# Hybrid decoder trunk on one core: 16 of the 22 inner tiles of the FFN down projection by seven block products, with parts of the inner layer worked out in the up projection and kept in DRAM

## The chip, the core and the metric

The kernel runs on one core of a Trainium2 chip. The core has a matrix engine (TensorE, PE in the profile; its weight loads are listed apart as PEld), VectorE (DVE), ScalarE (ACT), GpSimd (POOL), and SyncE (SP), which here issues nearly all DMAs, in order, from one queue. Each engine takes its own instructions strictly in the order in which the built program has them, and waits on semaphores for others. The metric is the device time of one execution in microseconds (us).

## What is computed

One decoder layer on 1024 tokens of width 1024: three token mixers in parallel with a merge and an output projection, and then the sub-layer that the change touches, the gated MLP:

```python
h = rms_norm(x, pre_ffn_norm[l])
u = causal_dwconv(h @ ffn_w_up[l], ffn_conv_w[l], ffn_conv_b[l])
gate, val = jnp.split(u, 2, axis=-1)
f = (jax.nn.gelu(gate, approximate=True) * val) @ ffn_w_down[l]
x = x + rms_norm(f, post_ffn_norm[l])
```

The inner width is 11 x 1024 / 4 = 2816, that is 22 tiles of 128 channels. Everything is float32.

## The kernel before

Activations stand with channels on partitions and tokens along the free axis, in two halves of 512 tokens (h = 0, 1). A float32 product is made of three matmuls: each operand is split into a rounded high part and the rest (`hi`, `lo`), and hi x hi, hi x lo and lo x hi are summed in PSUM. A split of an activation is a copy on ACT (`hi`) and a subtraction on DVE (`lo`); a split of a weight has its subtraction on POOL.

**Up projection.** Each inner tile f needs a gate tile and a value tile. The first four tiles go by plain products (`up_half`). For the other 18, `up_pair` takes gate and value tile (two blocks of output channels) by two token halves and two halves of the contraction as a 2 x 2 block product, and makes it with seven block products for eight (Winograd's form of Strassen's scheme): `weights7` works out sums of weight blocks on POOL and splits them on ACT and POOL, `product` issues the 12 matmuls of one of the seven, `snap` copies an intermediate PSUM bank to SBUF on ACT. The sums of the input blocks were made once before (`combos`). One pair is 84 matmuls. Then `conv` (three taps, ACT and DVE), GELU on ACT, and `gated` (DVE) make one inner tile of 128 x 512 for each token half, which is stored to DRAM (`m_d`, line 1528).

**Down projection.** Inner tiles come back from DRAM in chunks of 4, 4, 4, 4, 2 and 4 (`DOWN`). `m_split` loads a tile into a staging buffer (lines 1589 and 1595) and splits it (1601, 1602); `down` makes, for each of the eight output tiles j and both token halves, the plain product over the chunk's tiles, with weights from `load_w` (270 to 273), and adds the PSUM bank to one of 16 sums in SBUF (`acc`, line 1617; the first chunk copies, 1615). The last chunk is done by token ranges, with the final norm and residual.

The first chunk's tiles are loaded inside the last pair. The recorded program is put into its final order by a scheduler that goes by modelled times: it interleaves products of neighbouring pairs and stages, and gives each engine its fixed order. A buffer of a pool is taken in the order in which the program asks for it, once its last reader has been placed. PSUM has six banks for these stages (`dense`).

Of the kernel before, what the change touches and what calls it, by code (L numbers as in the profile page):

```python
# [23 lines left out]
NFF = 22  # L24
# [68 lines left out]
def layout(a):  # L93
# [31 lines left out]
    for i, (c0, c1) in enumerate(TM_CHUNKS):  # L125
# [15 lines left out]
    dn = g["ffn_w_down"]  # L141

    dns = [units(dn[c * 128:(c + n) * 128], ar(DM)) for c, n in DOWN]
    out.update(
        xT=np.ascontiguousarray(x.T), wfm=wfm, pv=np.ascontiguousarray(pv),
# [7 lines left out]
        wb_nsa=units(g["w_br_nsa"], ar(DM)), wo=units(g["w_out"], ar(DM)),  # L153
        wup=units(up, fch), **{f"wdn{i}": d for i, d in enumerate(dns)})
# [29 lines left out]
W_BUFS = (3, 4, 4)  # L184
U_BUFS = 4
OSQ = 6

N_FIRST = 4
# [1168 lines left out]
def tail_stage(nc, tc, es, env):  # L1357
# [152 lines left out]
    def snap(ps):  # L1510
        s = up_.tile([128, 512], F32, name="snap", bufs=5)
        act(s, ps, AF.Copy)
        return s

    m_d = E.scratch("m_d", [NFF * 128, T])

    def conv(u, h, ps, st):
# [3 lines left out]
        st[s, h] = up_.tile([128, 512], F32, name=f"u{s}")  # L1521
        E.conv(st[s, h], h, ps, [pvc(PV_FW, 3 * u + 2 - d) for d in range(3)], pvc(PV_FB, u), st["halo", s])
        if s == 0:
            act(st[0, h], st[0, h], AF.Gelu_apprx_tanh)

    def gated(f, h, st):
        V.tensor_tensor(st[0, h], st[0, h], st[1, h], op=OP.mult)
        nc.sync.dma_start(m_d[f * 128:(f + 1) * 128, hs(h)], st[0, h])

# [7 lines left out]
    def up_pair(f, rhs, between=None):  # L1537
# [7 lines left out]
        V.tensor_tensor(y, y, s1, op=OP.add)  # L1545
        conv(2 * f, 0, y, st)
        E.product(x, w, rhs, 6, False)
        s2 = snap(x)
# [9 lines left out]
        conv(2 * f + 1, 0, z, st)  # L1558
        gated(f, 0, st)
        E.product(x, w, rhs, 3, False)  # L1560
        conv(2 * f + 1, 1, s7, st)
# [9 lines left out]
    rhs = {q: [None] * 4 for q in range(1, 8)}  # L1571
    later = []
    for k in range(4):
        quarters = [(1, h2[0, k]), (2, h2[0, k + 4]), (3, h2[1, k + 4])]
        lows = [rows[0][k], rows[1][k], rows[0][k + 4], rows[1][k + 4]]
        E.combos(*lows, V)
        for q, b in quarters:
            rhs[q][k] = b
        t2, t1, t4, t3 = lows
        for q, t in ((6, t2), (7, t3)):  # L1580
            rhs[q][k] = hi, lo = x_t(), x_t()
            act(hi, t, AF.Copy)
            V.tensor_tensor(lo, t, fl(hi), op=OP.subtract)
        later += [(5, k, t1, hi_t), (4, k, t4, lo_t)]

    for q, k, t, place in sorted(later, key=lambda x: (-x[0], x[1])):
        rhs[q][k] = hi, lo = place(), x_t()
# [4 lines left out]

    def m_tile(f, h, s):
        t = x_t(F32) if s is None else up_.tile([128, 512], F32, name=f"u{s}")
        nc.sync.dma_start(t, m_d[f * 128:(f + 1) * 128, hs(h)])
        return t

    def m_split(f, h):
        src = m_tile(f, h, None if f < DOWN[0][1] else f % 2)
        hi, lo = hi_t(), lo_t()  # L1600
        act(hi, src, AF.Copy)
        V.tensor_tensor(lo, src, fl(hi), op=OP.subtract)
        return hi, lo

# [3 lines left out]
    def down(ci, f0, nf, ms):  # L1608
        end = None
        for j in range(8):  # L1610
            pss = fm_unit(psd, load_w(A[f"wdn{ci}"][j], nf * 128), lambda k, h: ms[f0 + k, h], nf)
            for h, ps in enumerate(pss):
                a = acc[h][j]
                if ci == 0:
                    act(a, ps, AF.Copy)
                else:
                    end = V.tensor_tensor(a, a, ps, op=OP.add)
        return end


    ms0 = {}
    for f in range(N_FIRST, NFF):
        up_pair(f, rhs, (lambda: ms0.update(m_chunk(*DOWN[0]))) if f == NFF - 1 else None)

    last = len(DOWN) - 1
    tc.keep_in_program_order(nc.scalar.preload_act_table_set(E.TABLE))
    for ci, (f0, nf) in enumerate(DOWN[:last]):
        if ci == 0:
            acc = [[x_t(F32) for _ in range(8)] for _ in range(2)]
        i = down(ci, f0, nf, m_chunk(f0, nf) if ci else ms0)  # L1630
        if ci == last - 2:
            late = i

# [4 lines left out]
    def w_split(j, place):  # L1638
        ws.append(load_w(A[f"wdn{last}"][j], 512, place, up_.tile([128, 512], F32, name="snap", bufs=5)))

# [16 lines left out]
    def norm_rows(ss, W):  # L1657
# [6 lines left out]
        E.rsqrt_mean(rt[:, :n], v[:, :n], ps[:, :n], DM)  # L1664
        rb = up_.tile([128, 512], F32, name="u1")
        act(rb[:, :W].rearrange("p (n t) -> p n t", t=128), rt[:, :n, None].to_broadcast([128, n, 128]), AF.Copy)
# [14 lines left out]
    for s0, s1 in LAST:  # L1681
        h = s0 // 512
        s = slice(s0 - h * 512, s1 - h * 512)
        W = s1 - s0
        ss = up_.tile([128, 512], F32, name="u0")
        for j in range(8):
# [10 lines left out]
            else:  # L1697
                sq = up_.tile([128, 512], F32, name="snap", bufs=5)
                act(sq[:, :W], a, AF.Square)
# [23 lines left out]
```

## Time and profile before

| | us |
|---|---|
| time, median of 3 runs (2288.70 to 2292.17) | 2292.13 |
| the profiled execution | 2297.28 |
| its span, first to last instruction | 2295.5 |
| mean granted TensorE clock in it (share of full speed) | 0.985 |
| PE busy in the span | 2197.3 |
| DVE, ACT, POOL busy | 1346.2, 1164.9, 1184.5 |

The up projection's pairs run from about 1690 to 2040 us of the span, the down projection from about 2000 to the end; the two overlap in the last pair. A row of groups has the line, the engine, the operation, what it writes and reads by the program's names, the shapes and the count, then busy time in us, the mean duration of one in ns, and the idle time of the engine just before such instructions, with what ended it. A row of the timeline or of the chain of waits begins with the start and the duration in us. In rows of windows, each engine has its busy time and, in brackets, its instructions; then the granted clock, the busy share of the DMA engines and GB/s.

### The profile page before, as it was taken

What the parts mean: (1) busy time and instruction counts of PE and PEld (TensorE: products, weight loads), DVE (VectorE), ACT (ScalarE), POOL (GpSimd) and SP (SyncE); (2) the same over time, 40 slices, a digit from 0 to 9 for tenths busy, and PEclk for the clock granted to TensorE, in tenths of its full rate; (3) what the DMA queues carried; (4) which work ended last, traced back from release to release, by engine and by line L of the source; (5) the groups of instructions that cost most, each with busy time, mean ns of one, the idle gap of its engine ahead of it and who ended that gap; (6) DMA issues with size and microseconds to landing.
All of it is one profiled execution on the core that took longest, in us unless ns stands there. A gap on an engine that the chain in (4) does not pass through costs nothing.

```text
span 2295.5 us, 29758 instructions
## 1 busy us (share of the span) xinstructions
PE 2197.3 (96%) x10663; PEld 1755.3 (76%) x10663; DVE 1346.2 (59%) x2376; ACT 1164.9 (51%) x2185; POOL 1184.5 (52%) x853
## 2 busy tenths in 40 slices
PE   7999999998999999999999999999899999999997
PEld 7878889865665678878775678887678888878886
DVE  7765554268567526556536653359876777744346
ACT  6544443466756646667755421245545555553124
POOL 3676741246736733333347655446578888822213
PEclk9999999999999999999999999999999999999998
DMA  4233341320221011112253253334322222264212
GB/s 170 81 111 108 116 132 62 112 70 24 62 67 31 12 56 42 60 65 93 83 211 112 80 213 129 119 128 162 106 79 86 85 83 83 84 223 130 93 32 74
DMA packets 115349, 222.03 MB, mean 97 GB/s; under 512 B 28160, under 2 KB 42432, under 8 KB 115200
## 3 DMA queue, kind: packets, MB, share of 16 engines
q1 hardware_dynamic: 112608, 217.80, 28.0%
q10 hardware_dynamic: 2592, 2.32, 0.3%
q8 instruction: 84, 1.38, 0.2%
q14 instruction: 65, 0.53, 0.1%
HBM read 162.80 MB, written 57.28 MB: 96 GB/s over the span
## 4 chain that ended last, share of the span: by engine, by line
PE 77%; DVE 11%; ACT 5%; issue 3%; DMA 3%; POOL 2%; SPq 0%; DVEq 0%; ACTq 0%; POOLq 0%
PE dense L208 55%; PE ps_s L208 7%; PE ps_o L208 6%; PE ps_t L208 6%; PE ps_b L208 4%; POOL wlo L273 1%; DVE x L1484 1%; DVE mx L938 1%; DVE u L310 1%; DVE osq L1457 1%; DVE x L1589 1%; DMA wraw<-in_wdn 1%; DMA wraw<-in_wfm 0%; DVE x L1677 0%; DMA x<-in_xT 0%
## 5 line engine op out<-in xcount | busy, mean ns | idle before, releaser
L273 POOL TENSOR_TENSOR wlo<-wraw,whi 128x1024 fp32r<-128x1024 f32 (+2 forms) x134 | 266.5, 1989 | 444.1 <-ACT whi L272 435.4
L208 PE MATMUL dense<-hi,whi 128*128 128x512 f32 x816 | 308.2, 392 | 4.8 <-ACT whi L272 4.8
L208 PE MATMUL dense<-hi,wlo 128*128 128x512 f32 x752 | 289.3, 394 | 8.9 <-POOL wlo L273 7.9
L208 PE MATMUL dense<-lo,whi 128*128 128x512 f32 x688 | 269.3, 392 | 0.5 <-POOL lo L1497 0.5
L208 PE MATMUL dense<-h_hi,whi 128*128 128x512 f32 x656 | 263.8, 402 | 0.0
L208 PE MATMUL dense<-h_lo,whi 128*128 128x512 f32 x656 | 257.5, 393 | 0.0
L208 PE MATMUL dense<-h_hi,wlo 128*128 128x512 f32 x656 | 257.2, 392 | 0.0
L272 ACT ACTIVATE whi<-wraw 128x1024 fp32r<-128x1024 f32 (+2 forms) x134 | 116.1, 867 | 277.4 <-PE dense L208 228.8
L976 POOL TENSOR_TENSOR wT_lo<-wT,wT_hi 128x512 fp32r<-128x512 f32 x132 | 168.5, 1288 | 101.3 <-ACT wT_hi L975 93.2
L208 PEld LDWEIGHTS dense<-hi,whi 128*128 128x128 f32 x816 | 154.2, 189 | 39.5 <-ACT whi L272 6.9
L208 PE MATMUL dense<-x,uhi 128*128 128x512 f32 x552 | 177.3, 392 | 3.9 <-ACT x L584 2.4
L208 PEld LDWEIGHTS dense<-hi,wlo 128*128 128x128 f32 x752 | 142.1, 189 | 41.7 <-POOL wlo L273 10.4
L208 PEld LDWEIGHTS dense<-lo,whi 128*128 128x128 f32 x688 | 130.0, 189 | 28.6 <-POOL lo L1497 1.4
L208 PEld LDWEIGHTS dense<-h_hi,wlo 128*128 128x128 f32 x656 | 123.7, 189 | 26.7
L208 PEld LDWEIGHTS dense<-h_hi,whi 128*128 128x128 f32 x656 | 124.4, 190 | 23.8
L208 PEld LDWEIGHTS dense<-h_lo,whi 128*128 128x128 f32 x656 | 124.3, 189 | 22.5
L1180 POOL TENSOR_TENSOR s_lo<-sa,s_hi 128x512 fp32r<-128x512 f32 (+2 forms) x48 | 53.5, 1115 | 152.1 <-ACT s_hi L1179 152.1
L938 DVE TENSOR_REDUCE mx<-ps_t 128x1 f32<-128x384 f32 (+3 forms) x192 | 98.7, 520 | 47.7 <-PE ps_t L208 44.0
L208 PEld LDWEIGHTS dense<-x,uhi 128*128 128x128 f32 x552 | 103.7, 189 | 27.5 <-ACT x L584 3.6
L965 ACT ACTIVATE wT<-ps_s 128x512 f32<-128x512 f32 x132 | 78.4, 594 | 72.4 <-PE ps_s L208 67.1
L310 DVE SCALAR_TENSOR_TENSOR u<-dense,pv,u 128x510 f32<-128x510 f32 (+1 forms) x140 | 101.9, 737 | 7.8 <-ACT u L306 7.6
L521 POOL TENSOR_TENSOR ulo<-uf,uhi 128x1024 fp32r<-128x1024 f32 x30 | 72.5, 2418 | 63.4 <-ACT uhi L520 63.4
(514 smaller groups left out, 5690.9 us busy)
## 6 DMA issues: line engine op xcount, KB each, us to landing
wraw<-in_wfm SPq DMA_DIRECT2D x62, 512.0 KB, 3.7
wraw<-in_wup SPq DMA_DIRECT2D x52, 512.0 KB, 3.7
g_d<-gate_e SPq DMA_DIRECT2D x48, 256.0 KB, 2.1
s_d<-o SPq DMA_DIRECT2D x48, 256.0 KB, 2.0
ge<-g_d SPq DMA_DIRECT2D x24, 512.0 KB, 3.5
m_d<-u SPq DMA_DIRECT2D x44, 256.0 KB, 2.0
u<-m_d SPq DMA_DIRECT2D x36, 256.0 KB, 4.0
row<-s_d SPq DMA_DIRECT2D x16, 512.0 KB, 4.2
```

The costliest lines, as they stand in the source:

```text
L208: i = f(*a, **k)
L272: act(hi, raw, AF.Copy)
L273: (V if tiles else P).tensor_tensor(lo, raw, fl(hi), op=OP.subtract)
L310: V.scalar_tensor_tensor(o[:, d:], ps[:, :512 - d], taps[d], o[:, d:], op0=OP.mult, op1=OP.add)
L521: P.tensor_tensor(l24, f24, fl(h24), op=OP.subtract)
L938: V.tensor_reduce(mx[:, h, a, n:n + 1], pm[:, :w], axis=AX, op=OP.max)
L965: act(w.rearrange("p h q -> p (h q)"), pz, AF.Exp)
L976: P.tensor_tensor(lo, wf, fl(hi), op=OP.subtract)
L1180: (P if SB_SLO else V).tensor_tensor(s_lo[:, c0:], a[:, c0:], fl(s_hi[:, c0:]), op=OP.subtract)
L1457: eng.tensor_tensor(sums[0], sums[0], sq, op=OP.add)
L1484: e.tensor_tensor(o[j], o[j], x, op=OP.add)
L1589: V.tensor_tensor(lo, t, fl(hi), op=OP.subtract)
```

## The change

The inner tiles 4 to 19 are taken in four chunks of four tiles by seven block products each (`DOWN7`); the tiles 20, 21 and then 0 to 3 stay with plain products (`DOWN`). A chunk is worked in two halves of four output tiles (d = 0, 1). In a half, the 2 x 2 blocks are: two groups of output channels, two groups of contraction (even and odd inner tiles), and the two token halves. Weights are prepared by the same `weights7` as in the up projection, from a regrouped copy of the weight matrix, once per half.

The right-hand blocks of two neighbouring inner tiles (an even and an odd one, two token halves) have seven forms: three are tiles of the inner layer themselves, and four are differences and sums of them. `combine` works these four out on DVE in the up projection, after each odd tile, in two steps that are put off into the next pair, and stores them; the DRAM array `m7_d` holds seven blocks per two tiles for 16 tiles. `m_sets` loads and splits them in the order in which the products use them, straight into the buffer of the low part (`split_to`), without a staging buffer. Two sets of seven, one for each two tiles, make a chunk; of every third set, five of the seven blocks go to the pool `x`, which also holds the 16 sums.

`down7` issues, for each of the seven products and two output tiles, six matmuls, and adds the bank to one of the sums at once, one addition per product and bank; banks of three kinds (x, y, z; two each) keep running sums as in the scheme, so a bank is read by DVE and then written on. In the first chunk, the first write of each sum is a copy on ACT.

Counted in the built programs, PE has 96 matmuls fewer, DVE 104 instructions more, ACT 24, POOL 32 and the queue of SP 32 DMAs more. Buffers: `u0` 6 and `u1` 2 for 4 each, snapshots 6 for 5.

```diff
-DOWN = [(0, 4), (4, 4), (8, 4), (12, 4), (16, 2), (18, 4)]
+DOWN7 = [4, 8, 12, 16]
+DOWN = [(20, 2), (0, 4)]
...
+ORDER7 = (1, 2, 6, 7, 5, 4, 3)
...
     def gated(f, h, st):
-        V.tensor_tensor(st[0, h], st[0, h], st[1, h], op=OP.mult)
-        nc.sync.dma_start(m_d[f * 128:(f + 1) * 128, hs(h)], st[0, h])
+        m = st[0, h]
+        V.tensor_tensor(m, m, st[1, h], op=OP.mult)
+        if not in_pairs(f):
+            nc.sync.dma_start(m_d[f * 128:(f + 1) * 128, hs(h)], m)
+            return
+        if f % 2 == 0:
+            even[h] = m
+            q = {0: 1}.get(h)
+        else:
+            q = 2 + h
+        p = (f - DOWN7[0]) // 2
+        if q:
+            nc.sync.dma_start(m7_rows(p, q), m)
+        if f % 2 and h:
+            later.extend(combine(p, even[0], even[1], st[0, 0], m))
...
+    def combine(p, b11, b12, b21, b22):
+        t7, t6, t4 = [up_.tile([128, 512], F32, name="snap", bufs=SNAPS) for _ in range(3)]
+        def one():
+            V.tensor_tensor(t7, b12, b22, op=OP.subtract)
+            V.tensor_tensor(b12, b11, b12, op=OP.subtract)
+            for q, t in ((7, t7), (5, b12)):
+                nc.sync.dma_start(m7_rows(p, q), t)
+        def two():
+            V.tensor_tensor(t6, t7, b11, op=OP.subtract)
+            V.tensor_tensor(t4, t6, b21, op=OP.add)
+            for q, t in ((6, t6), (4, t4)):
+                nc.sync.dma_start(m7_rows(p, q), t)
...
+    def split_to(hi, lo, src):
+        nc.sync.dma_start(fl(lo), src)
+        act(hi, fl(lo), AF.Copy)
+        V.tensor_tensor(lo, fl(lo), fl(hi), op=OP.subtract)
+        return hi, lo
+    def m_sets(c):
+        sets = [{}, {}]
+        for n, q in enumerate(ORDER7):
+            for i, st in enumerate(sets):
+                if (2 * c + i) % 3 == 2 and n < 5:
+                    hi, lo = x_t(), x_t()
+                else:
+                    hi, lo = hi_t(), lo_t()
+                st[q] = split_to(hi, lo, m7_rows(2 * c + i, q))
+        return sets
+    def down7(c, sets):
...
+        for d in range(2):
+            w = E.weights7(wx, A[f"wds{c}"][d, 0], A[f"wds{c}"][d, 1], 512)
+            x, y, z = [[bank(), bank()] for _ in range(3)]
...
+            for q, ps, start, outs in ((1, x, True, ((0, 0, OP.add, True),)),
+                                       (2, y, True, ((0, 0, OP.add, False),)),
+                                       (6, x, False, ((0, 1, OP.subtract, True),)),
+                                       (7, z, True, ((1, 1, OP.add, True),)),
+                                       (5, x, False, ((1, 1, OP.subtract, False),)),
+                                       (4, z, False, ((0, 1, OP.add, False),)),
+                                       (3, x, False, ((1, 0, OP.add, True),))):
+                for n in range(2):
+                    product2(ps[n], q, n, start)
+                    for h, m, op, first in outs:
+                        end = add(h, 4 * d + 2 * n + m, ps[n], op, first)
```

More of the change, by code (lines that the diff above doesn't have):

```diff
@@ L1510, in snap @@
     def snap(ps):
-        s = up_.tile([128, 512], F32, name="snap", bufs=5)
+        s = up_.tile([128, 512], F32, name="snap", bufs=SNAPS)
         act(s, ps, AF.Copy)
@@ L1571, in tail_stage @@
     rhs = {q: [None] * 4 for q in range(1, 8)}
-    later = []
+    parts = []
     for k in range(4):
@@ L1591, in tail_stage, with split_in @@
     acc = []
[L1593 to L1596, printed above, removed]
-    def m_split(f, h):
[L1599 to L1603, printed above, removed]
+    def split_in(src):
+        hi, lo = hi_t(), lo_t()
+        return split_to(hi, lo, src)
@@ L1613, in down @@
                 a = acc[h][j]
[L1614 to L1621, printed above, removed]
-    for f in range(N_FIRST, NFF):
-        up_pair(f, rhs, (lambda: ms0.update(m_chunk(*DOWN[0]))) if f == NFF - 1 else None)
+                V.tensor_tensor(a, a, ps, op=OP.add)
+    acc = [[], []]
+    sets = []
+    for f in range(N_FIRST, NFF):
+        up_pair(f, rhs, (lambda: sets.extend(m_sets(0))) if f == NFF - 1 else None)
+    tc.keep_in_program_order(nc.scalar.preload_act_table_set(E.TABLE))
+    for c in range(len(DOWN7)):
+        if c:
+            sets = m_sets(c)
+        late = down7(c, sets)
     last = len(DOWN) - 1
-    tc.keep_in_program_order(nc.scalar.preload_act_table_set(E.TABLE))
     for ci, (f0, nf) in enumerate(DOWN[:last]):
[L1628 to L1632, printed above, removed]
+        down(ci, f0, nf, m_chunk(f0, nf))
     f0, nf = DOWN[last]
@@ L1638, in w_split @@
     def w_split(j, place):
-        ws.append(load_w(A[f"wdn{last}"][j], 512, place, up_.tile([128, 512], F32, name="snap", bufs=5)))
+        ws.append(load_w(A[f"wdn{last}"][j], 512, place, up_.tile([128, 512], F32, name="snap", bufs=SNAPS)))
     for k in range(nf):
```

57 lines of the change are left out of this document (49 added, 8 removed).

## The prediction

> **What bounds the kernel now.** I read first the page, then the windows over the feed-forward part, then the chain of waits in order of time, then who TensorE (PE) waits for.
>
> ```profile
> span 2295.5 us, 29758 instructions
> ```
> ```profile
> core 0: us, PE busy (x) PEld busy (x) DVE busy (x) ACT busy (x) POOL busy (x), PEclk, DMA share, GB/s
> 1950.00:2000.00 50.00, 50.00 (x222) 41.42 (x221) 33.90 (x45) 28.09 (x41) 40.86 (x24) 1.00 0.25 85
> 2000.00:2020.00 20.00, 16.96 (x68) 13.50 (x67) 14.44 (x21) 9.44 (x17) 12.86 (x9) 0.91 0.40 136
> 2050.00:2100.00 50.00, 47.56 (x209) 38.75 (x208) 18.21 (x27) 21.71 (x39) 11.64 (x9) 1.00 0.67 231
> ```
> ```profile
> 1699.38 293.12 PE dense L208 x1284
> ...
> 2007.08 3.52 DMA x<-m_d
> 2010.75 0.46 issue
> 2011.21 0.59 ACT snap L1512
> 2011.85 36.36 PE dense L208 x153
> ...
> 2049.62 11.88 DMA wraw<-in_wdn
> ```
> ```profile
> PE dense L208 <- ACT snap L1512: 5.1, 2, 3.0
> PE dense L208 <- ACT whi L272: 2.3, 1, 2.3
> ```
>
> In the up projection (1699 to 2012) and the down projection (to 2264) PE has no idle time in most windows. Only two stops show from 2000 on. At 2008.8 PE waits 3.0 us: a load of an inner tile is late, ScalarE (ACT), in order, takes the snapshot behind that tile's split. That window's granted clock is 0.91, so 0.09 x 20 = 1.8 us more are lost. In the window from 2050, after 36 inner-tile loads at once, a weight load takes 11.88 us and 13 of 222 matmuls are missing: 2.9 us. So fewer matmuls is the right thing to buy, if nothing else becomes late.
>
> **The price of a matmul.** One pair of the up projection is 84 matmuls and strictly periodic:
>
> ```profile
> 1897.12 0.39 PE L208 MATMUL dense<-hi,uhi 128*128 128x512 f32 x1
> 1916.16 0.39 PE L208 MATMUL dense<-hi,uhi 128*128 128x512 f32 x1
> 1918.88 0.61 PE L208 MATMUL dense<-x,uhi 128*128 128x512 f32 x2
> ```
> 19.04 us / 84 = 0.2267 us each (the 0.39 of a row overlaps its neighbours).
>
> **The change part by part.**
>
> *Removed:* 16 inner tiles cost 16 x 8 x 2 x 3 = 768 matmuls; seven products cost 4 chunks x 2 halves x 84 = 672. 96 x 0.2267 = **-21.8 us**, all on PE's path.
>
> *The weight-load stop after 2049* came from 36 loads in a burst; now the second half's weights load during the last pair and seven loads are spread over each half of 19 us, so I let it go: **-2.9** (bounds -2.9, and 0 if a burst comes back).
>
> *Weights.* 32 preparations of 128x512 become eight of the up projection's kind. VectorE (DVE) and GpSimd (POOL) rows of the up projection and the down projection:
>
> ```profile
> L310 DVE SCALAR_TENSOR_TENSOR u<-snap,pv,u 128x510 f32<-128x510 f32 x16 | 44.8, 2797 | 0.0
> L524 POOL TENSOR_TENSOR ulo<-uf,uhi 128x1024 fp32r<-128x1024 f32 x16 | 38.9, 2434 | 17.2 <-ACT uhi L523 17.2
> L521 POOL TENSOR_TENSOR ulo<-uf,uhi 128x1024 fp32r<-128x1024 f32 x16 | 38.4, 2400 | 27.7 <-ACT uhi L520 27.7
> L512 POOL TENSOR_TENSOR wlo<-wraw,whi 128x1024 fp32r<-128x1024 f32 x15 | 36.1, 2404 | 0.0
> L312 DVE SCALAR_TENSOR_TENSOR u<-halo,pv,u 128x2 f32<-128x2 f32 x31 | 35.8, 1156 | 0.0
> L310 DVE SCALAR_TENSOR_TENSOR u<-dense,pv,u 128x510 f32<-128x510 f32 x46 | 33.8, 735 | 0.0
> L522 POOL TENSOR_TENSOR uf<-wraw 128x512 f32<-128x512 f32 x16 | 28.0, 1748 | 0.0
> L517 POOL TENSOR_TENSOR uf<-wraw 128x512 f32<-128x512 f32 x16 | 25.6, 1601 | 1.2
> L519 POOL TENSOR_TENSOR uf<-uf,wraw 128x512 f32<-128x512 f32 x16 | 25.6, 1598 | 1.3
> L1527 DVE TENSOR_TENSOR u<-u,u 128x512 f32<-128x512 f32 x30 | 25.3, 843 | 1.8 <-ACT u L1524 0.4
> L526 POOL TENSOR_TENSOR alo<-wraw,ahi 128x512 fp32r<-128x512 f32 x16 | 20.8, 1302 | 0.0
> ```
> ```profile
> L1617 DVE TENSOR_TENSOR x<-x,dense 128x512 f32<-128x512 f32 x44 | 30.2, 687 | 71.8 <-PE dense L208 71.7
> L1602 DVE TENSOR_TENSOR lo<-u,hi 128x512 fp32r<-128x512 f32 x24 | 17.0, 748 | 11.3 <-ACT hi L1601 11.3
> ```
> POOL per half: 2.43 + 2.40 + 2.40 + 1.75 + 1.60 + 1.60 + 1.30 (L526) and once more for the sum of the same size (L518) = 14.8 us of 19.04. The up projection carries these and one more subtraction in the same time and PE is never short of weights there, so: 0. The cover is PE's own work on the half before; POOL has 4.2 us to spare, and what it took beyond that PE would pay in full, in each of eight halves.
>
> *DVE in the down projection.* A half has 14 adds from PSUM (a chunk of four tiles, twice a half's time and more, had 16; in the first chunk ACT makes 8 of 14 as copies) and about 7 splits: 14 x 0.69 + 7 x 0.69 = 14.5 us of 19.04, before waits. The waits are the question. The row L310 u<-snap takes 2.80 us where the same work from PSUM takes 0.74, and the timeline shows why:
>
> ```profile
> 1900.96 2.40 POOL L524 TENSOR_TENSOR ulo<-uf,uhi 128x1024 fp32r<-128x1024 f32 x1 [1.16 <-ACT uhi L523]
> ```
> ```profile
> 1900.27 0.21 DVE L312 SCALAR_TENSOR_TENSOR u<-halo,pv,u 128x1 f32<-128x1 f32 x1
> ...
> 1901.06 2.84 DVE L310 SCALAR_TENSOR_TENSOR u<-snap,pv,u 128x510 f32<-128x510 f32 x1
> ...
> 1909.97 1.02 DVE L1527 TENSOR_TENSOR u<-u,u 128x512 f32<-128x512 f32 x1
> 1914.86 0.70 DVE L1545 TENSOR_TENSOR dense<-dense,snap 128x512 f32<-128x512 f32 x1 [3.88 <-ACT snap L1512]
> ```
> The DVE operation with both inputs in SBUF ended half a microsecond after POOL's. Per pair such operations lose 2.06 (L310) + 2 x 0.95 (L312, 1.16 against 0.21) + 2 x 0.15 (L1527, 0.84 against 0.69) = 4.3 us. A split has both inputs in SBUF too; an add from PSUM has not. With the same 4.3 us, a half costs DVE 18.8 of 19.04 us: 99%. The order of instructions leaves 19 to 24 matmuls (4.3 to 5.4 us) between a bank's last matmul and its next, which absorbs most; I take 0.7 us per half over the six halves after the first chunk: **+4** (bounds: 0, as in the up projection, and, if each of seven splits waited 2.06, 9.8 x 6 = 59).
>
> The Trainium skill ("SBUF — State Buffer", section "Who interferes with whom") says that a VectorE instruction with two SBUF inputs and a GpSimd instruction that reads SBUF exclude each other, the later one blocked until the first ends. By that rule, these rows agreeing, it speaks against this change, and it is the second rival below.
>
> *Parts of the inner layer, in the up projection.* Per two pairs: four DVE operations (two SBUF inputs, 4 x 0.69 = 2.8 us) and three more stores. They stand right after the odd pair's second L1527, where DVE idles 3.88 us. What they make late: a snapshot buffer is now held until the store of the first part has landed, and the next pair's first snapshot waits for it on ACT, with the rest of ACT's work behind it. From 1910.99: wait for POOL 1.2, operation 0.6, issue 0.4, landing 2.0 to 4.0 (rows below), snapshot 0.6: 1915.8 to 1917.8; PE needs it at 1918.88. So 0 (bounds 0 and 8 x 1 us).
>
> ```profile
> m_d<-u SPq DMA_DIRECT2D x44, 256.0 KB, 2.0
> u<-m_d SPq DMA_DIRECT2D x36, 256.0 KB, 4.0
> ```
> Stores 44 to 68, loads of inner tiles 44 to 68, weights the same bytes in 16 loads: 7 x 256 KB + 2 x 512 KB per half is 2.8 MB in 19 us, 150 GB/s, where the windows show 231 served. The store of the parts goes ahead of a weight load on the DMA queue of SyncE (SP), 1.5 us at most; that load has more than 4 us of lead. ACT gets 24 instructions more, and is at 28 of 50 us: 0, as long as no load holds it up in order.
>
> *The stop at 2008.8 remains.* The first sets are loaded straight into freed tiles, no longer through two spare ones, but the last of these eight loads stands on SP's queue behind two stores of parts. From the end of L1527 (1910.99 in the cycle): two splits and two parts, 2.8; store and load issue 0.7; landing 2.6 to 4; split, weights and snapshot on ACT 0.63 + 1.06 + 0.58. That is 9.4, and PE wants the snapshot 5.2 us after (1916.16): about 4.0 idle for 3.0, with the clock loss as before: **+1.0** (bounds -4.8, it vanishes, and +4).
>
> *A new stop after the first chunk.* The third set keeps five of seven products' inputs in the tiles that also hold the 16 sums, and in the order of instructions their loads come after all sums are first written; on SP they are queued behind a load that waits for the first chunk's last but one matmul, and the next chunk's first matmul needs them. The path is that of 2007.08 to 2011.85, 4.8 us, and two issues (0.7) and DVE's split with the two ahead of it (1.5 to 2): **7.0 idle, 1.8 of clock: +8.8** (bounds 4.8, that path bare, and 13.2, the 11.88 us load and a split).
>
> The Trainium skill ("TensorE: Matmul & The Clock Gate", section "HAM oscillation — how this bites in real kernels") puts the halved clock behind idle stretches of more than about 3.4 us. The row above shows 0.91 after 3.0 us, so I charge it to both stops; by the page's bound the stop of before would have lost none, and the first of these two terms would be 2.8 for 1.0.
>
> **Sum:** -21.8 - 2.9 + 4 + 1.0 + 8.8 = -10.9. The profiled execution is 2297.28 us (span 2295.5 and 1.8 around it), 5.15 above the median 2292.13. 2297.3 - 10.9 = 2286.4; against the median, 2281.
>
> **Rivals.**
> 1. Most stops hide: the third set's loads land fast (4.8 + 1.8) and DVE keeps up (0): -21.8 - 2.9 + 1.0 + 6.6 = -17.1, 2275; with the 2008.8 stop gone too, 2269. For it: PE stayed busy in the up projection with POOL's load as high. Against: DVE was 68% busy there (33.90 of 50).
> 2. Slower: DVE becomes the bound in the down projection, because its splits and POOL's weights block each other. If a split waits 1.2 us on average instead of 0.6, a half takes 9.7 + 7 x 1.9 = 22.9 us, 3.9 over PE's: six halves 23 instead of 4, so -10.9 + 19 = +8: 2300. It decides from 1.0 us per split. For it: 2.80 us rows. Against: L1602 in the down projection now takes 0.75 (POOL only 23% busy there).
> 3. Snapshots in the up projection wait for stores, 1 to 2 us in each of eight: 2289 to 2297. Against: 1 to 3 us of room, above.
>
> **How the numbers follow.** Forecast (2274 to 2288) 0.5; rival 1, 0.2; rival 2 in full 0.12, and half of it (2288 to 2297) 0.1; rival 3, 0.08. A measurement tells about 0.2%, 4.6 us, from no change. Faster by more: 0.5 + 0.2, so 0.70; within: half of rival 2 and most of rival 3, 0.16; slower: 0.14. The range leaves out rival 2 in full and the best corner of rival 1: 2267 to 2296.
>
> **What would show it.** Right: 96 fewer matmuls; PE full in the up projection, period 19.04; one stop of 6 to 8 us some 38 us into the seven products, ended by ACT or DVE on a tile loaded from the parts, with the granted clock dipping there; DVE near 95% busy in the halves. Wrong: PE idle before adds from PSUM in every half, L1695 or the splits long (rival 2); snapshot waits every second pair (rival 3); no stop after the first chunk (rival 1).

## The result, and the profile after

The changed kernel takes 2296.99 us (median of 10 runs, 2292.19 to 2299.45), the kernel before 2289.38 (10 runs, 2285.99 to 2292.55): ratio 1.0028, 95% interval 1.0018 to 1.0038, so 4 to 9 us slower. The prediction was 2281, in a range of 2267 to 2296.

The spans of the two profiles, 2295.5 and 2295.6, don't show this, because the profiled execution of before was late ahead of the change already: its stretch of pairs starts 4.64 us later. The chain of waits does, from the first full stretch of the pairs to the first matmul of the last norm. In before that stretch starts at 1699.38 (row in the prediction). Its end, and then both ends in after:

```profile
2259.18 0.78 PE psn L208 x8
```
```profile
1694.74 26.32 PE dense L219 x107
...
2259.21 0.79 PE psn L219 x8
```

559.80 us before, 564.47 after: 4.67 us longer, with 96 matmuls fewer. (The ratio of the medians says 6.4 us; these are two single executions, and 4.67 lies inside the interval.) The windows of after (columns as in the prediction: busy us and instructions of PE, PEld, DVE, ACT, POOL, then the granted clock, the DMA share and GB/s):

```profile
1950.00:2000.00 50.00, 49.76 (x220) 40.85 (x219) 38.77 (x50) 26.70 (x38) 41.40 (x24) 1.00 0.31 101
2000.00:2020.00 20.00, 17.08 (x73) 13.15 (x72) 18.02 (x29) 12.03 (x20) 12.00 (x8) 1.00 0.61 212
2020.00:2050.00 30.00, 26.74 (x116) 21.16 (x115) 24.83 (x31) 17.50 (x29) 24.71 (x14) 1.00 0.56 201
2050.00:2100.00 50.00, 39.30 (x154) 29.79 (x154) 41.51 (x42) 25.48 (x39) 34.57 (x18) 0.90 0.46 158
2100.00:2150.00 50.00, 48.04 (x208) 38.42 (x207) 41.48 (x49) 18.84 (x26) 33.36 (x18) 1.00 0.36 121
2150.00:2200.00 50.00, 48.50 (x212) 39.21 (x211) 40.79 (x51) 17.41 (x26) 31.91 (x19) 1.00 0.37 117
```

PE is full in none of them. The large hole is 2050 to 2100, where 154 matmuls run in place of some 220. Whom PE waited for from 1690 to 2256 (total us, times, longest):

```profile
PE dense L219 <- ACT snap L1523: 6.6, 11, 2.0
PE dense L219 <- DVE x L1695: 5.9, 7, 1.3
PE dense L219 <- ACT x L1661: 5.1, 1, 5.1
PE dense L219 <- DVE x L1662: 2.8, 1, 2.8
PE dense L219 <- ACT uhi L534: 1.6, 1, 1.6
PE dense L219 <- DVE u L321: 1.5, 1, 1.5
PE dense L219 <- ACT whi L283: 1.4, 1, 1.4
PE dense L219 <- POOL ulo L535: 0.2, 1, 0.2
```

25.1 us in 24 stops, where before had 7.6 in 4. A stop costs more than its wait, as the timeline shows at one of the eleven behind a snapshot, for PE and for ACT:

```profile
1811.77 0.39 PE L219 MATMUL dense<-hi,wlo 128*128 128x512 f32 x1
1812.39 0.50 PE L219 MATMUL dense<-hi,uhi 128*128 128x512 f32 x1 [0.24 <-ACT snap L1523]
1812.73 0.40 PE L219 MATMUL dense<-x,uhi 128*128 128x512 f32 x1
```
```profile
1810.57 1.29 ACT L1537 ACTIVATE u<-u 128x512 f32<-128x512 f32 x2 [5.09 <-DVE u L323]
1811.77 1.06 ACT L1523 ACTIVATE snap<-dense 128x512 f32<-128x512 f32 x2
```

Two matmuls take 0.96 us from start to start for 0.45: 0.51 lost for a wait of 0.24. So the account below goes by starts: what lies between two starts beyond 0.2267 us, summed for each place over the timeline's matmul rows, slow matmuls after a stop included (eight of 0.43 us after 2087). The rows of the table make 33.0 less 7.9, that is 25.1 (the same as the waits by chance), and -21.8 + 25.1 = +3.3; the chain has +4.7. So 1.4 us stay without a place; some 1.0 of them are delays of under 0.03 us each, too small for a row.

| Place in after | Lost, us | Same place before |
|---|---|---|
| pairs, every second one, 7 stops behind a snapshot | 3.6 | 0 |
| 2005 to 2014, 3 stops behind a snapshot | 3.7 | 4.9 (stop at 2008.8) |
| 2038 to 2056, first chunk, 5 stops | 4.8 | 0 |
| 2071 and 2074, end of the first chunk, behind additions | 3.1 | 0 |
| 2077 to 2092, before and in the second chunk | 10.9 | 0 |
| 2123 to 2179, 7 stops, most behind additions | 5.3 | 0 |
| weights of the plain chunks (2059 before, 2222 after) | 1.6 | 3.0 |

VectorE's splits and additions from 2040 to 2200, by shape (count, busy us, mean ns):

```profile
L1662 DVE TENSOR_TENSOR lo<-lo,hi 128x512 fp32r<-128x512 f32 x43 | 57.5, 1358 | 6.8 <-ACT hi L1661 6.8
L1695 DVE TENSOR_TENSOR x<-x,dense 128x512 f32<-128x512 f32 x86 | 56.0, 679 | 19.2 <-PE dense L219 18.9
L1662 DVE TENSOR_TENSOR x<-x 128x512 fp32r<-128x512 f32 x10 | 12.5, 1254 | 0.2
```

A split takes 1.32 us on average, (57.5 + 12.5) / 53, where L1602 took 0.75 before. An addition from PSUM stays at 0.68. The timeline of VectorE and that of GpSimd, ahead of two of the stops (PE starts again at 2136.74 and 2138.44):

```profile
2130.57 0.68 DVE L1662 TENSOR_TENSOR lo<-lo,hi 128x512 fp32r<-128x512 f32 x1
2131.17 1.27 DVE L1695 TENSOR_TENSOR x<-x,dense 128x512 f32<-128x512 f32 x2
2132.36 3.73 DVE L1662 TENSOR_TENSOR lo<-lo,hi 128x512 fp32r<-128x512 f32 x2
2136.01 0.68 DVE L1695 TENSOR_TENSOR x<-x,dense 128x512 f32<-128x512 f32 x1
```
```profile
2131.45 2.40 POOL L535 TENSOR_TENSOR ulo<-uf,uhi 128x1024 fp32r<-128x1024 f32 x1 [1.35 <-ACT uhi L534]
2133.92 1.62 POOL L528 TENSOR_TENSOR uf<-wraw 128x512 f32<-128x512 f32 x1
```

The split at 2130.57 runs while GpSimd is idle and takes 0.68 us. The next two take 3.73 together: the second ends at 2136.09, 0.55 after GpSimd's operation, and only then comes the addition for which PE waits. The 68 splits of L1662 in the trace are all of these two kinds: 34 took 0.68 to 0.69 us, among them all 28 that had no GpSimd operation beside them; the other 34 took more than 0.8, and each of these ended 0.55 to 0.56 us after a GpSimd operation did.

### The profile page after: what moved, and what is told of

It is laid out like the page before. It is cut to its first block, busy times and chain, and to the rows that moved or that the text cites. A ratio compares the mean times of both kernels' runs of the same rounds, so it can differ in the third digit from the quotient of the medians.

```text
span 2295.6 us, 29819 instructions
## 1 busy us (share of the span) xinstructions
PE 2180.8 (95%) x10567; PEld 1732.9 (75%) x10567; DVE 1461.5 (64%) x2480; ACT 1190.0 (52%) x2209; POOL 1263.5 (55%) x885
## 3 DMA queue, kind: packets, MB, share of 16 engines
q8 instruction: 83, 1.36, 0.2%
## 4 chain that ended last, share of the span: by engine, by line
PE 72%; DVE 14%; ACT 6%; issue 4%; DMA 2%; POOL 1%; SPq 0%; DVEq 0%; ACTq 0%; POOLq 0%
PE dense L219 49%; PE ps_s L219 7%; PE ps_o L219 6%; PE ps_t L219 6%; PE ps_b L219 4%; DVE u L321 2%; DVE u L323 1%; DMA lo<-m_d 1%; DVE lo L1662 1%; POOL wlo L284 1%; DVE mx L949 1%; DVE x L1495 1%; DVE osq L1468 1%; DVE x L1650 1%; DVE x L1786 0%
## 5 line engine op out<-in xcount | busy, mean ns | idle before, releaser
L284 POOL TENSOR_TENSOR wlo<-wraw,whi 128x1024 fp32r<-128x1024 f32 (+2 forms) x102 | 223.8, 2195 | 322.5 <-ACT whi L283 278.1
L219 PE MATMUL dense<-hi,whi 128*128 128x512 f32 x608 | 227.8, 393 | 6.3 <-ACT whi L283 3.8
L219 PE MATMUL dense<-hi,wlo 128*128 128x512 f32 x544 | 213.7, 397 | 9.0 <-POOL wlo L284 8.3
L219 PE MATMUL dense<-x,uhi 128*128 128x512 f32 x600 | 192.2, 392 | 3.9 <-ACT x L595 2.4
L219 PE MATMUL dense<-lo,whi 128*128 128x512 f32 x480 | 188.3, 393 | 0.2 <-DVE lo L1510 0.2
L283 ACT ACTIVATE whi<-wraw 128x1024 fp32r<-128x1024 f32 (+2 forms) x102 | 95.8, 940 | 170.7 <-PE dense L219 134.7
L532 POOL TENSOR_TENSOR ulo<-uf,uhi 128x1024 fp32r<-128x1024 f32 x38 | 92.2, 2427 | 89.4 <-ACT uhi L531 86.1
L219 PEld LDWEIGHTS dense<-hi,whi 128*128 128x128 f32 x608 | 115.3, 190 | 34.5 <-ACT whi L283 5.8
L219 PEld LDWEIGHTS dense<-hi,wlo 128*128 128x128 f32 x544 | 103.2, 190 | 33.7 <-POOL wlo L284 10.3
L535 POOL TENSOR_TENSOR ulo<-uf,uhi 128x1024 fp32r<-128x1024 f32 x38 | 97.8, 2574 | 53.1 <-ACT uhi L534 50.4
L219 PE MATMUL dense<-hi,uhi 128*128 128x512 f32 x248 | 99.7, 402 | 12.7 <-ACT snap L1523 6.4
```

What stands on the lines that cost most here:

```text
L219: i = f(*a, **k)
L283: act(hi, raw, AF.Copy)
L284: (V if tiles else P).tensor_tensor(lo, raw, fl(hi), op=OP.subtract)
L532: P.tensor_tensor(l24, f24, fl(h24), op=OP.subtract)
L535: P.tensor_tensor(l31, f31, fl(h31), op=OP.subtract)
```

## Experiments

All edits are to the changed kernel. Each run stands against runs of the kernel before on the same chip, whose median was 2288 to 2291 us; so the ratio is what to compare. The changed kernel has 1.0028, and 0.001 is 2.3 us.

**1. Only the loads of the third set earlier.**

```diff
+    def load_ahead():
+        for q in ORDER7[:5]:
+            ahead[q] = x_t(), x_t()
+            nc.sync.dma_start(fl(ahead[q][1]), m7_rows(2, q))
...
+                if d == 1:
+                    load_ahead()
                 for n in range(4):
                     for h in range(2):
                         acc[h].append(x_t(F32))
```

> Of the changed kernel, only this is changed: the five pairs of x tiles of the third set are asked for, and their loads issued, before the second half of the first chunk asks for its eight sums, and not after. Theory A (what holds the first matmuls of the second chunk is where these loads stand in the order: in the changed kernel the fourth-last stop, 5.1 us of idle for ACT x L1661 and 2.8 for DVE x L1662, with the granted clock at 0.90 in 2050 to 2100, some 10 us together): the loads issue 15 to 20 us earlier, the two waits on x tiles are gone, the clock stays at 1.00, and the kernel takes 2296.99 - 10 = 2287, a little under the kernel before. Rival B (VectorE is behind there anyway, the late loads only show it): waits on the lo tiles or on the additions of L1695 take the place of the stop, and less than 3 us is gained.

Measured: 2299.22 us, ratio 1.0045 (1.003 to 1.0059), no gain. The stop stays, 3.3 us for ACT and 7.4 for DVE, though the five loads were issued some 19 us ahead of it. Waits of PE, and the timeline of SP's queue and of VectorE:

```profile
PE dense L219 <- DVE x L1684: 7.4, 1, 7.4
...
PE dense L219 <- ACT x L1683: 3.3, 1, 3.3
```
```profile
2058.16 2.43 SPq L1673 DMA_DIRECT2D x<-m_d  x5
```
```profile
2079.73 7.58 DVE L1662 TENSOR_TENSOR lo<-lo,hi 128x512 fp32r<-128x512 f32 x4
2087.24 4.15 DVE L1684 TENSOR_TENSOR x<-x 128x512 fp32r<-128x512 f32 x5
```

The loads had moved, the splits not: VectorE still makes the x splits after those of the other set. Theory A failed as put, but the run does not decide between it and B.

**2. Loads and splits earlier, without and with the splits from PSUM of experiment 4.**

```diff
-            ahead[q] = x_t(), x_t()
-            nc.sync.dma_start(fl(ahead[q][1]), m7_rows(2, q))
+            ahead[q] = split_to(x_t(), x_t(), m7_rows(2, q))
```

> As e1_x_early, but the five splits of the third set's x blocks are asked for early too, with their loads, so that they stand ahead of the splits of the fourth set on ScalarE and VectorE (in e1_x_early only the loads were moved, and TensorE waited 3.3 us for ACT x and 7.4 us for DVE x). Theory A, mended (the order of loads and splits makes the stop): no stop over 2 us between 2060 and 2110, the clock stays at 1.00, 8 to 10 us under the changed kernel: 2287 to 2289. Rival B (VectorE is late whatever the order, because GpSimd holds up its splits): the wait moves to the lo splits or to the additions, under 3 us gained, 2294 to 2297.

> e13_loads_splits_early with the splits of the seven-product chunks from PSUM, as in e9_psum_split. If the order and the shutting out are two causes, their gains add: as e69_place_psum, 2280 to 2286, with TensorE at 48 of 50 us or more in each window from 2050 on. If only one of them counts, this one takes no less time than the better of e9_psum_split (2291.3) and e13_loads_splits_early.

Measured: 2294.31, ratio 1.0018 (1.0008 to 1.0029), and 2291.93, 1.0005 (0.9992 to 1.0017); the first can't be told from the changed kernel, nor the second from experiment 4 alone. Neither theory of the first run holds: the stop is gone from where the second chunk begins and stands inside the first chunk instead. The chain of waits of the first run there:

```profile
2067.30 4.08 DMA lo<-m_d
...
2071.47 0.63 ACT hi L1661
...
2073.32 0.49 ACT x L1703
...
2073.86 4.33 PE dense L219 x12
```

At 2067.30 PE gives back a lo tile; only then can the block for it be loaded; ACT, in order, holds that block's copy, the x copies and, behind them, an eviction of the first chunk (L1703), for which PE waits 6.4 us. With the splits from PSUM the same stop is 8.3 us. So what makes this stop is that blocks of the next chunk go into tiles that the present chunk is just giving back, with ACT's evictions queued behind them. Moving the other blocks' loads did not remove it.

**3. Other tiles for the same blocks.**

```diff
-                if (2 * c + i) % 3 == 2 and n < 5:
+                p = 2 * c + i
+                if p % 3 == 1 and n >= 2:
```

> Of the changed kernel, one rule is changed: the five blocks that go to the x pool are the last five of every second set of three (the first chunk's second set first), not the first five of every third. So the first chunk's late blocks come into x tiles that the last pair gives back early, and the second chunk's first set goes to hi and lo tiles that the last pair gives back. Theory A (order of asking): the stop before the second chunk's first matmul goes, and the stops of 2039 to 2056 (some 5 us, ACT behind loads of the first chunk's last blocks) become smaller: 10 to 15 us gained, 2282 to 2287. Rival B (VectorE is behind there anyway): the stop only moves, under 3 us gained. Rival F: the new first chunk waits for x tiles (the sixth and seventh product of the last pair free them late), and loses 2 to 6 us of the 10.

Measured: 2291.56, ratio 1.001 (0.9998 to 1.0021): about 4 us gained of the 10 to 15 expected (the interval overlaps a little with that of the changed kernel). The windows and a wait row:

```profile
2050.00:2100.00 50.00, 48.72 (x213) 39.38 (x212) 42.01 (x46) 25.30 (x40) 40.47 (x22) 1.00 0.45 143
2100.00:2150.00 50.00, 45.80 (x186) 36.24 (x185) 39.73 (x47) 16.64 (x24) 34.20 (x19) 0.93 0.41 133
```
```profile
PE dense L219 <- DVE x L1696: 7.5, 10, 2.0
```

The stop is gone, 213 matmuls run where 154 did, and the clock stays at 1.00. But the next window is worse than in after: PE now waits for VectorE's additions, 7.5 us for 5.9. The large stop had also given VectorE time to catch up, it seems. That is rival B, but only in part, since some gain stays.

**4. The splits of the seven-product chunks read one input from PSUM.**

```diff
+    def split_ps(hi, lo, src=None):
+        if src is not None:
+            nc.sync.dma_start(fl(lo), src)
+        ps = psn.tile([128, 512], F32, name="psn", tag="psn")
+        act(ps, fl(lo), AF.Copy)
+        act(hi, fl(lo), AF.Copy)
+        V.tensor_tensor(lo, ps, fl(hi), op=OP.subtract)
+        return hi, lo
...
-                st[q] = split_to(hi, lo, m7_rows(2 * c + i, q))
+                st[q] = split_ps(hi, lo, m7_rows(2 * c + i, q))
```

> Of the changed kernel, only the splits of the seven-product chunks are changed: ScalarE copies a loaded block to one of the two PSUM banks that lie idle here, beside the copy to the high part, and VectorE subtracts the high part from that bank, so that it reads one input from SBUF and one from PSUM. Count and size of VectorE's instructions, GpSimd's work and the loads stay; ScalarE has one copy of 0.6 us more per split. Theory C (two SBUF inputs on VectorE and GpSimd's operations shut each other out, and this is what makes VectorE late): the split takes 0.69 to 0.75 us in place of 1.27 with GpSimd as busy as before, the waits for L1695 go (8 us), of the stop before the second chunk the 2.8 us of DVE go and the 5.1 us of ACT x L1661, a late load, stay; 8 to 12 us gained, 2285 to 2289. Rival D (the count of VectorE's instructions, or GpSimd's work delaying the weights): the splits or the waits stay as they are, under 3 us gained. Rival I (ScalarE becomes late with 14 more copies a chunk): waits for ACT take their place.

Measured: 2291.32, ratio 1.0001 (0.9988 to 1.0013): some 6 us gained, under the 8 to 12 expected. VectorE's splits from 2040 to 2200, a wait row, and a window:

```profile
L1671 DVE TENSOR_TENSOR lo<-psn,hi 128x512 fp32r<-128x512 f32 x38 | 25.6, 685 | 9.3 <-ACT hi L1670 6.9 <-ACT psn L1669 2.4
```
```profile
PE dense L219 <- ACT x L1670: 6.9, 1, 6.9
```
```profile
2100.00:2150.00 50.00, 50.00 (x223) 41.39 (x222) 39.79 (x63) 30.26 (x50) 30.72 (x18) 1.00 0.40 121
```

Same instruction, same size, GpSimd with the same operations: 0.69 us for 1.32. Here 30 of the 56 splits from PSUM had a GpSimd operation beside them, and none of them took more than 0.69. So with both inputs in SBUF the two engines shut each other out, like a lock that only one can hold, and with one input in PSUM they don't. Of the 5.9 us of waits for additions 0.8 is left, and PE is full from 2100 to 2150. The stop before the second chunk stays, as expected (6.9 us, ACT), and two around the end of the last pair grow (2.2 us for a snapshot, 4.4 for weights that ACT copies), where ACT has more to do: so rival I holds in part, which fits the smaller gain. Theory C holds, D falls.

**5. GpSimd's four additions of weight blocks left out, alone and with the early loads of experiment 1.**

```diff
-        P.tensor_tensor(u1, a21, a22, op=OP.add)
-        P.tensor_tensor(u2, u1, a11, op=OP.add)
-        P.tensor_tensor(u4, u2, a12, op=OP.add)
+        if sums:
+            P.tensor_tensor(u1, a21, a22, op=OP.add)
+            P.tensor_tensor(u2, u1, a11, op=OP.add)
+            P.tensor_tensor(u4, u2, a12, op=OP.add)
+        else:
+            f31, f24 = raws
...
-        P.tensor_tensor(u3, a11, a21, op=OP.add)
+        if sums:
+            P.tensor_tensor(u3, a11, a21, op=OP.add)
```

> Of the changed kernel, the seven-product chunks leave out the four additions of weight blocks that GpSimd makes for each half (u1, u2, u4, u3), and the splits that follow take raw blocks in their place; so the result is not the reference's. The up projection keeps them. GpSimd then has 4 operations of 8 to 9 us in a half of 19 us instead of 8 of 14.8. Theory C (splits on VectorE are stretched by GpSimd's operations; the row L1662 shows 1.27 us where 0.69 is its time alone): L1662 falls to 0.9 to 1.0 us in the chunks, the waits of TensorE for L1695 (5.9 us in 7 stops, with what follows each some 8 us) go down by half or more, and 4 to 7 us are gained. Rival D (VectorE has too many instructions in a half, whatever their length, or the order gives the additions too little room): L1662 gets shorter, but the waits for L1695 stay, and under 2 us are gained.

> Of the changed kernel: the third set's loads early, as in e1_x_early, and GpSimd's four additions of weight blocks left out, as in e4_no_sums (so the result is not the reference's). Theory J (the stop before the second chunk has two causes that stand behind one another, the late loads and VectorE; each alone keeps it up: with early loads it was 3.3 + 7.4 us for ACT x and DVE x, without the sums 5.6 us for ACT x): with both gone there is no stop over 2 us between 2060 and 2110 and the granted clock stays at 1.00; 2286.89 - 8 = 2279. Rival K (something third holds the second chunk, such as the loads of the lo tiles): a stop of 4 us or more stays there, 2284 or more.

Measured: 2286.89, ratio 0.9986 (0.9976 to 0.9996), and 2289.79, 0.9995 (0.9983 to 1.0008). VectorE's splits in the first of them, and a window:

```profile
L1666 DVE TENSOR_TENSOR lo<-lo,hi 128x512 fp32r<-128x512 f32 x47 | 46.0, 992 | 13.4 <-ACT hi L1665 13.1
```
```profile
2100.00:2150.00 50.00, 50.00 (x221) 41.14 (x220) 43.31 (x55) 21.18 (x31) 23.10 (x10) 1.00 0.49 156
```

With half of GpSimd's operations gone, VectorE's splits, untouched, fall to 0.99 us and PE waits for no addition. It is the other side of the same lock. About 10 us are gained; that this is more than in experiment 4 is within the noise. In this window VectorE is busy 43.3 of 50 us, more than in after (41.5), and yet PE doesn't wait: it is not VectorE's share of busy time that stops PE, but long splits ahead of an addition. In the second run the stop stays (4.6 us for ACT, 3.1 for DVE): theory J fell, probably for the reason that experiment 2 then showed.

**6. Four of a chunk's 14 subtractions moved to GpSimd, on top of experiment 3.**

```diff
-                st[q] = split_to(hi, lo, m7_rows(2 * c + i, q))
+                st[q] = split_to(hi, lo, m7_rows(2 * c + i, q), P if c and n % 3 == 1 else V)
```

> The place rule of e6_place, and of the 14 splits of a chunk after the first four (those of the products 2 and 5) have their subtraction on GpSimd and not on VectorE. It takes 4 x 1.28 = 5.1 us a chunk from VectorE (38 us of work for TensorE) and adds 4 x 1.3 to GpSimd, which has 14.8 us of work in 19. Theory C (shutting out): VectorE and GpSimd together do not get room, since each operation of the one that reads SBUF twice still holds up the other: 0 to 5 us gained on e6_place, 2287 to 2291. Rival D (VectorE has too much to do, counted in instructions): four fewer of 42 a chunk take most of the waits for L1696 away, 6 to 8 us gained, 2284 to 2286.

Measured: 2292.69, ratio 1.0005 (0.999 to 1.0019), not to be told from experiment 3 alone. The splits left on VectorE take 1.3 us as before. From 2050 to 2100 VectorE is busy 33.4 us for 42.0 in experiment 3, but PE still waits 6.5 us for additions (7.5), and more for GpSimd's weights (2.0 us for 1.2). Sharing the work between two engines that shut each other out gained nothing that can be told from noise; D falls again.

**7. The order on ScalarE in the pairs.**

```diff
         conv(2 * f, 0, y, st, True)
-        deferred()
         E.product(x, w, rhs, 6, False)
         s2 = snap(x)
+        with tc.issue_after(last[0].ins):
+            gelus()
+        deferred()
```

(`conv`, called with True, no longer issues the GELU of a gate tile; `gelus` issues those of this pair's first half and of the last pair's second, and then the last pair's `gated`.)

> Of the changed kernel, only the order on ScalarE in the up projection is changed: in every pair the second snapshot stands ahead of the two GELUs, as it stands in the kernel before; in the changed kernel it stands behind them in every second pair, where TensorE stops for 0.24 us and its next matmuls start late, 0.5 us of the 38.61 us that two pairs take. Theory G (this order alone costs it): two pairs take 38.08 us again, 8 times 0.5 = 4 us gained, 2293. Rival H (the four operations of VectorE for the parts, or their stores, cost it): two pairs stay at 38.6, another wait takes the place, and nothing is gained.

Measured: 2302.9, ratio 1.0061 (1.0047 to 1.0075): 8 us slower than the changed kernel. A window of the pairs in after, and in this kernel:

```profile
1800.00:2000.00 200.00, 198.80 (x872) 162.99 (x871) 160.18 (x208) 103.26 (x146) 165.12 (x94) 1.00 0.31 102
```
```profile
1800.00:2000.00 200.00, 200.00 (x884) 165.62 (x883) 168.42 (x211) 104.34 (x148) 170.01 (x96) 1.00 0.32 102
```

In the pairs theory G holds: with the snapshot ahead of the GELUs the stops are gone, 884 matmuls for 872, with the parts and their stores still there. But all of it, and more, is lost later: 3.4 us at 2007 behind a snapshot, 2.7 at 2052 behind the last pair's convolution on VectorE, and 9.9 in place of 7.9 before the second chunk. Where the first chunk is late anyway, arriving there earlier gives no time. That it took 8 us more was not expected; the places are read off the stops, and no further run shows the cause.

**8. Together.** First experiments 3 and 4; then, with the splits of the plain chunks from PSUM too, the order of experiment 7; then in its place another order on ScalarE in the first chunk; then both.

```diff
     def split_in(src):
         hi, lo = hi_t(), lo_t()
-        return split_to(hi, lo, src)
+        return split_ps(hi, lo, src)
...
-        if between:
-            between()
...
         s3 = snap(x)
+        if between:
+            with tc.issue_after(last[0].ins):
+                between()
...
             w = E.weights7(wx, A[f"wds{c}"][d, 0], A[f"wds{c}"][d, 1], 512)
+            if (c, d) == (0, 0):
+                with tc.issue_after(E.weights7.ahi.ins):
+                    m_sets(0, sets, slice(4, 7))
```

> The place rule of e6_place and the splits from PSUM of e9_psum_split together, nothing left out. If the two causes are separate (the order of the loads, and VectorE and GpSimd shutting each other out), the gains add: e6_place is 5.4 us under the changed kernel with 7.5 us of waits for L1696 and some 4 us of slow clock left, so 2291.6 - 8 to 12 = 2280 to 2284, 5 to 9 us under the kernel before. If the stops only move, it stays at 2288 or more.

> e69_place_psum, with the splits of the plain chunks taken from PSUM too (12 of them took 1.39 us there) and the order of e8_gelu in the up projection (the second snapshot ahead of the GELUs). Theory L (e8_gelu lost on the whole because VectorE, still late in the first two chunks, gave nothing back: its stops from 2050 to 2090 were 20 us in place of 13): with VectorE relieved the 4 us of the up projection stay gained, and 1 to 2 us of the waits for L1705: 2286.4 - 4 to 6 = 2280 to 2282. Rival M (the order itself does harm at the end of the up projection: in e8_gelu TensorE stopped for 3.4 us at 2007 behind a snapshot that stands behind the split of a late block, 1.1 us before): that stop stays and takes 2 to 5 us back, 2283 to 2289.

> e69_place_psum, with the splits of the plain chunks from PSUM too, and with ScalarE's order changed at two places: the copies of the first eight blocks of the first chunk stand behind the last pair's third snapshot, and those of its last six blocks behind the last copy of the first chunk's weights; before that they stood ahead, and ScalarE, in order, held snapshots and weights while a block's load was on its way. Theory N (the stops between 2006 and 2055, in e69_place_psum 2.3, 0.7, 1.4, 1.1, 0.7, 2.5 and 0.9 us, come from this order): 4 to 7 us of these 9.6 go, 2279 to 2282. Rival O (the loads themselves are late, and the first chunk's products wait for them wherever the copies stand): the stops only get other names (a split for a snapshot), under 2 us gained, 2284 to 2287.

> e11_act_order and the order of e8_gelu together. If theories L and N hold, the gains add: 2274 to 2278, 13 to 17 us under the kernel before. If M or O holds, 2280 to 2286.

| | us | ratio | 95% interval |
|---|---|---|---|
| place and splits from PSUM | 2286.43 | 0.9989 | 0.9975 to 1.0003 |
| and the order in the pairs | 2282.74 | 0.9971 | 0.9958 to 0.9984 |
| the order in the first chunk instead | 2289.07 | 0.9994 | 0.9983 to 1.0005 |
| both orders | 2284.87 | 0.998 | 0.9967 to 0.9994 |

Place and PSUM add: 4 and 6 us alone, about 9 together. With them, the order in the pairs, which lost 8 us alone, loses nothing: the time is 4 us lower, but the two intervals overlap, and the splits of the plain chunks were changed in the same run. In the profile the pairs keep the gain, 884 matmuls from 1800 to 2000 for 871 without this order. This kernel is the fastest, 4 to 10 us under the kernel before. Its windows:

```profile
2020.00:2050.00 30.00, 24.28 (x99) 19.02 (x98) 25.66 (x35) 20.26 (x35) 18.23 (x11) 0.94 0.61 205
2050.00:2100.00 50.00, 49.49 (x218) 40.40 (x217) 29.53 (x44) 36.46 (x63) 38.16 (x23) 1.00 0.49 162
2100.00:2150.00 50.00, 50.00 (x222) 41.30 (x221) 32.70 (x53) 28.97 (x48) 35.41 (x21) 1.00 0.47 154
```

From 2050 to 2150 PE is full but for half a microsecond; VectorE is at 29.5 of 50 us where it was at 41.5. What is left is the passage from the last pair to the first chunk. The other order there, with the block copies behind snapshots and weights, gave nothing (rival O): the same window got worse,

```profile
2020.00:2050.00 30.00, 18.83 (x61) 13.75 (x61) 22.28 (x30) 27.85 (x48) 18.98 (x12) 0.77 0.68 237
```

PE then waits for the splits of those blocks (6.4 us). ACT, with two copies a block, is busy 27.9 of 30 us there, and the chain ahead of the first of these splits goes through its copies and the convolution, not through a load. So rival O is right that the stops only change their names, but late loads as the reason are not shown.

## Why the prediction was wrong

What bounds the kernel was read rightly, and the price of a matmul: 96 x 0.2267 = 21.8 us were saved. They were all spent again. The sum missed by 14.2 us. The largest step that failed is that the first chunk, from 2038 us on, was given no cost at all: 7.9 us were lost there (4.8 + 3.1). Next come the pairs, put at 0 (3.6), and then the sizes of the other terms. Term by term (predicted, measured by the account above, in us):

| Term | Predicted | Measured |
|---|---|---|
| matmuls | -21.8 | -21.8 |
| stop at the weights of a plain chunk | -2.9 | -1.4 |
| VectorE in the six halves after the first chunk | +4 | +5.3 |
| VectorE at the end of the first chunk | none | +3.1 |
| stop at 2008.8 | +1.0 | -1.2 |
| snapshots in the pairs | 0 | +3.6 |
| blocks of the first chunk after the last pair | none | +4.8 |
| stop after the first chunk | +8.8 | +10.9 |
| sum | -10.9 | +3.3 |

- **VectorE.** The mechanism was the one named, down to its size: 4.3 us a half were assumed for waits, 0.61 for each of seven splits, and 0.63 were found (1.32 less 0.69). In the six halves for which it was charged, 0.9 us a half came for the 0.7 of "which absorbs most; I take 0.7 us per half". What failed is where it was charged: "over the six halves after the first chunk" left out the first chunk's end, and there 3.1 us were lost behind additions. The sign "DVE near 95% busy in the halves" did not come either; it was busy 41 of 50 us. But ahead of each stop behind an addition it had had no idle time for 6.9 us or more, with stretched splits in front of the addition that PE needed. The cause is shown from both sides, by experiments 4 and 5. The Trainium skill ("SBUF — State Buffer", section "Who interferes with whom") says that a VectorE instruction with at most one SBUF input, outside its 2-port modes, does not contend with GpSimd; the 0.69 us of experiment 4 agree. The rule on two SBUF inputs, which the prediction named against this change, did count against it, but as a part of the loss and not as the whole of rival 2.
- **The stop after the first chunk.** It came where it was put, 7.9 us idle for 7.0. Its cause was put on SP's queue: "queued behind a load that waits for the first chunk's last but one matmul". In after that is what SP's queue shows: four loads of lo tiles until 2077.60, the first x load at 2077.65. But experiments 1 and 2 show that moving those loads, and the splits with them, only moves the stop. Experiment 3 shows what removes it: tiles that come free a chunk earlier.
- **The first chunk.** No term stood for the eight loads that the last pair's end sets free (2032 to 2039 us); only the first ones were costed, at the stop of 2008.8. Of the 4.8 us, 2.3 are behind a weight copy that ACT holds behind these blocks' copies, and what follows it, and 1.8 behind the last pair's convolution, which VectorE holds behind a split of 1.76 us. Experiment 8 shows that turning ACT's order round doesn't help. Whether the loads are too late there, or ACT has too much to do, stays open.
- **The pairs.** "So 0 (bounds 0 and 8 x 1 us)": the bounds held, the value not. And the reason was another: not a snapshot that waits for a store, but a second snapshot that the fixed order puts behind two GELUs in every second pair (experiment 7).
- **The range** left out "rival 2 in full" and ended at 2296. What came was a part of rival 2 and losses in three other places together; that the time still fell within the span given for its half (2288 to 2297) is chance. The terms had been summed as if they were independent, but the losses at VectorE, in the pairs, in the first chunk and after it all ended with ACT or VectorE being late in a fixed order, and so had one sign.

## What to carry to other kernels

Before matmuls are traded for additions and splits, look at what the work beside them does to VectorE and GpSimd at once: an operation of VectorE with two SBUF inputs took 1.32 us beside a busy GpSimd on average and 0.69 with one input in PSUM, with a copy on ScalarE as the price. Where buffers are reused, ask which tile a load must wait for and what stands behind its consumer on an in-order engine; moving other loads earlier in the queue did not help here while one tile was not free. Test fixes together as well as alone: one that lost 8 us alone lost nothing beside two others.

## What the runs showed of the hardware

The lock works both ways: GpSimd's additions of 128x512 (L528 to L530) took 1.53 to 1.68 us in after and 1.34 to 1.36 with the splits from PSUM, a gain for GpSimd that nothing had been done for.

```profile
L529 POOL TENSOR_TENSOR uf<-uf,wraw 128x512 f32<-128x512 f32 x7 | 11.7, 1678 | 0.0
```
```profile
L529 POOL TENSOR_TENSOR uf<-uf,wraw 128x512 f32<-128x512 f32 x7 | 9.5, 1361 | 0.0
```

These are the groups of after and of experiment 4, from 2040 to 2200. The low granted clock cost only what fell on running matmuls. The window from 2050 to 2100, at 0.90, would have lost 5 us by the prediction's reckoning (there 0.09 x 20 = 1.8). It held eight matmuls of 0.43 us and two of 0.59, some 2.2 us lost, near the 1.8 that the prediction charged; the rest of the slow time fell on idle PE.
